# SSD group norm by four 32-column products with a root on 128x128, and earlier weight splits for the third group

## The chip, the cores and the metric

The kernel runs on one core of a Trainium2 chip. The time is that of one execution in device microseconds (us). The core has a matrix engine (TensorE, PE in the profile; its weight loads are PEld), VectorE (DVE), ScalarE (ACT), GpSimd (POOL) and SyncE (SP), which issues most DMAs. Each engine works its own instructions in order; semaphores let one wait for another.

## The reference

A trunk of two layers on x (1, 512, 1024): a gated short convolution, then a Mamba-2 mixer (SSD), each followed by a SwiGLU feed-forward, each with RMS norms before and after and a shift, scale and gate from c. The change lies in the SSD mixer. Cut to what matters:

```
z, xbc, dt_raw = split(h @ w_in)
xbc = silu(causal_depthwise_conv(xbc, conv_w) + conv_b)
xs, bm, cm = split(xbc)                 # 2048 channels, 8 groups x 128 states, twice
y = ssd_chunked(xs, dt, a, bm, cm) + d_skip * xs
y = y * silu(z)
y = rms_normalize(y.reshape(b, s, 8, 256)).reshape(b, s, 2048) * norm_g
return y @ w_out
```

The last norm is taken for each token over the 256 channels of one group: y / sqrt(mean(y*y) + eps).

## The kernel before

Activations lie with channels on the 128 partitions and the 512 tokens along the row. A float32 product is made of three products in a rounded format: each weight block (128x1024, `whl`) is split into a high part (ACT, a cast, L202) and a low part (DVE, the difference, L203), and PE multiplies high by high, high by low and low by high (`mm3`, L259 to L261), 24 matmuls of 512 columns for a block.

The SSD stage runs over 8 groups (`Group`). A group needs six blocks of projections: two of x (wx0, wx1), one of B and one of C (wbc0, wbc1), two of z (wz0, wz1). `load_w` loads two blocks in one staging tile `wst` (two such tiles) and splits each into one of four `whl` buffers; a buffer is free again when PE has used the block. The products for B, C and x go through a convolution (`conv4`: ACT's bias step and DVE's three steps L957, both on `cu`, then ACT's silu, L959, which makes `xs`, `bt`, `ct`), those for z through a silu alone (`zs`).

What the mixer does with them is cut into steps. `step_a` transposes xs and B (PE: `xtok`, `btokp`; DVE: `xw`, `xdt`) and multiplies C by B (`cb`, masked to `cbm`). `states` makes the chunk states `st` and their running sum `prev`. `e_sub` and `e_fin` make the decays in `csb` (DVE subtractions L1067, ACT's exponential, DVE's product with `cbm`). `step_cc` makes the two parts of y (PE: `yo` from `prev`, `yd` from `csb`), which DVE adds and gates to `yg`; their squares are summed in `accg`. `step_d` is the norm: a product of a 128x128 matrix of ones with `accg` sums over the partitions (`ssg`, the same sum on all 128 partitions), ACT takes the root (L1119), DVE the reciprocal (L1120) and multiplies both `yg` of the group by it (L1123).

PSUM has four banks for projections (`ip`) and four for all else (`ssg`, `xtok`, `btokp`, `cb`, `st`, `yo`, `yd`).

PE's order is written by hand: in pass g of the loop, the blocks of group g+1 stand between the steps of group g. For the first group and the projections of the second, the orders of ACT and DVE are written by hand too; from there on a scheduler sets them, by the priorities that instructions have from their place in the program. What stands in `tc.high_priority()` is taken ahead of the rest. In the passage between the two regimes, ACT and DVE split the blocks of the third group (`Group(2)`) while they finish the first and second.

Of the kernel before, what the change touches and what calls it, by code (L numbers as in the profile page):

```python
# [8 lines left out]
F32 = mybir.dt.float32  # L9
F32R = mybir.dt.float32r  # L10
AF = mybir.ActivationFunctionType
# [5 lines left out]
P = 128  # L17
T = 512
D = 1024
KD = D // P  # L20
DFF = 2816
NF = DFF // P
DIN = 2048
NH = 32
HD = 64
NG = 8
NCH = 4
# [8 lines left out]
def trunk_kernel(  # L36
# [9 lines left out]
    act, dve, pe, pool = nc.scalar, nc.vector, nc.tensor, nc.gpsimd  # L46
# [3 lines left out]
    dram = ctx.enter_context(tc.tile_pool(name="dram", bufs=1, space=DRAM))  # L50

    tmp = ctx.enter_context(tc.tile_pool(name="tmp", bufs=4))
# [7 lines left out]
    def aux_ps(name, shape=(P, T)):  # L60
        return ps.tile(list(shape), F32, tag="aux", name=name, bufs=4)

    def t2(name):
        return tmp.tile([P, T], F32, tag="t2", name=name, bufs=4)
# [4 lines left out]
    ones = consts.tile([P, P], F32, name="ones")  # L69
# [3 lines left out]
    eps_t = consts.tile([P, 1], F32, name="eps")  # L73
# [127 lines left out]
    def split_w(src, dst, nk):  # L201
        act.copy(dst[:, 0, :nk, :], src)  # L202
        dve.tensor_tensor(dst[:, 1, :nk, :], src, dst[:, 0, :nk, :].bitcast(F32), SUB)  # L203

    def load_w(srcs, nk=KD, k0=0, later=None):


        st = wst_p.tile([P, 8, 256], F32, tag="wst", name="wst")
        o = 0
        for m, c0, n in srcs:  # L210
            dma(st[:, :nk, o:o + n], m[k0 * P:(k0 + nk) * P, c0:c0 + n].rearrange("(k p) f -> p k f", p=P))
            o += n
        res = []
        for b in range(o // P):
            w = whl_p.tile([P, 2, 8, P], F32R, tag="whl", name="whl")
            sw = st[:, :nk, b * P:(b + 1) * P]
            if later is None:
                split_w(sw, w, nk)
            else:
                later.append((lambda sw=sw, w=w: act.copy(w[:, 0, :nk, :], sw),  # L220
                              lambda sw=sw, w=w: dve.tensor_tensor(w[:, 1, :nk, :], sw,
                                                                   w[:, 0, :nk, :].bitcast(F32), SUB)))
            res.append(w)
        return res
# [317 lines left out]
    wm_in, wm_out = m_w_in[0], m_w_out[0]  # L542

    with ExitStack() as ph:
# [96 lines left out]
        with tc.manual_schedule(engines={PE_ENGINE, mybir.EngineType.SP, mybir.EngineType.Activation,  # L641
# [122 lines left out]
            for name in OPENING.split():  # L764
                step(name)
            later = []
            next_cv = [load_w([(w_in0, (i + 1) * D + 2 * P, 256)], later=later) for i in range(2)]
            for hi, lo in later:
                hi()
# [20 lines left out]
        for jp in range(0, KD, 2):  # L790
            if jp == 0:
                pss = lead_ps[:4]
            else:
                ws = next_cv[0] + next_cv[1] if jp == 2 else [
                    w for i in range(2) for w in load_w([(w_in0, (i + 1) * D + jp * P, 256)])]
                pss = [in_chunk(w, h) for w in ws]
            us = [conv_mix_cv(jp + b, pss[b], pss[2 + b]) for b in range(2)]
            wb = load_w([(w_in0, jp * P, 256)]) if jp else None
            for b in range(2):
                a = act_tile(f"bu{jp + b}")  # L800
                conv_mix_b(us[b], in_chunk(wb[b], h) if jp else lead_ps[4 + b], a)
                acts.append(a)
            ada_next(2 if jp < 6 else 0)
            if jp == 4:
                put_gates(0)
                gg = make_gg(0, gg_tile)
                other_vectors(actp.tile([P, 8, P], F32, tag="a", name="rows2"))
# [57 lines left out]
    with ExitStack() as ph:  # L865
# [4 lines left out]

        cs_d = dram.tile([NH, T], F32, name="cs_d")
        ecs_d = dram.tile([NH, T], F32, name="ecs_d")

        dt_tok = consts.tile([P, NH, NCH], F32, name="dt_tok")
        cs_tok = consts.tile([P, NH, NCH], F32, name="cs_tok")
# [89 lines left out]
        class Group:  # L965
# [8 lines left out]
            def weights(self, i, later=None):  # L974
                g = self.g
                if i == 0:
                    self.wx = load_w([(wm_in, DIN + g * 256, 256)], later=later)
                elif i == 1:
                    self.wbc = load_w([(wm_in, 2 * DIN + g * P, P), (wm_in, 2 * DIN + D + g * P, P)],
                                      later=later)  # L980
                else:
                    self.wz = load_w([(wm_in, g * 256, 256)], later=later)

            def conv(self, i, pst):
                g = self.g
# [127 lines left out]
            def step_d(self):  # L1113

                g = self.g
                pt = aux_ps("ssg")
                pe.matmul(pt, ones, self.accg, start=True, stop=True)
                rg = t2("rg")
                act.activation(rg, pt, AF.Sqrt, bias=eps_t, scale=1.0 / 256)  # L1119
                dve.reciprocal(rg, rg)  # L1120
                for q in range(2):
                    y = ygs[2 * g + q]
                    dve.scalar_tensor_tensor(y, y, mng[:, 2 * g + q:2 * g + q + 1], rg, MUL, MUL)  # L1123
# [26 lines left out]
        with tc.manual_schedule(engines={PE_ENGINE, mybir.EngineType.Activation, mybir.EngineType.DVE}):  # L1150
            cur, nxt = Group(0), Group(1)
            later = []
# [365 lines left out]
```

## Time and profile before

| | us |
|---|---|
| median of 3 runs | 1379.9 |
| lowest, highest | 1378.26, 1380.02 |
| profiled execution | 1378.87 |
| its span, first to last instruction | 1377.0 |

The SSD stage lies between about 630 and 970 us of the span. A row of a timeline is start, duration, engine, line, operation, output<-inputs, form and count; in square brackets stand the idle time before it and what ended that. A row of the waits is who waited for whom: us in total, times, longest. In the chain of waits a row is start, length, engine, tile, line and count. `L959` and the like are lines of the kernel before.

### The profile page before, as it was taken

The page shows a single profiled execution, that of the slowest core. Times are in us where ns is not written, and L with a number is a line of the kernel's source. Part 1 is how long each engine was busy: PE and PEld are TensorE (multiplying, and loading weights), DVE is VectorE, ACT ScalarE, POOL GpSimd, SP SyncE. Part 2 cuts the span into 40 slices and gives each one's busy share as a digit, 9 for nine tenths or more (in the row PEclk, how much of TensorE's full clock was granted, in tenths as well). Part 3 has the DMA queues.
Part 4 walks back from the last instruction along what each step waited for, and adds up shares of the span by engine and source line. Part 5 has one row for each costly group of instructions (what it writes and reads, how often), then busy time and mean ns, then how long its engine had stood idle before and what let it go on. Part 6 is the DMA issues. An engine that isn't in the chain of part 4 may idle for free.

```text
span 1377.0 us, 17627 instructions
## 1 busy us (share of the span) xinstructions
PE 1353.4 (98%) x6973; PEld 1136.3 (83%) x6973; DVE 911.3 (66%) x1485; ACT 580.2 (42%) x875; POOL 1.5 (0%) x11
## 2 busy tenths in 40 slices
PE   8999999999999999999899999999999999999997
PEld 7788889888888888898778888888889888887886
DVE  5777757478775222669879888787675655334877
ACT  4432247222222211665655656543473222223754
POOL 0000000000000000000000000000000000000000
PEclk9999999999999999999989999999999999999999
DMA  9956670467683322514444324332233986423743
GB/s 314 318 182 218 228 238 24 136 215 274 215 283 106 130 93 69 149 33 144 120 139 128 91 89 138 108 107 92 92 122 134 343 276 244 134 69 128 249 163 118
DMA packets 163702, 222.09 MB, mean 161 GB/s; under 512 B 7060, under 2 KB 112164, under 8 KB 161188
## 3 DMA queue, kind: packets, MB, share of 16 engines
q1 hardware_dynamic: 159616, 208.20, 46.2%
q10 hardware_dynamic: 4004, 12.77, 2.9%
q8 instruction: 55, 0.90, 0.3%
q14 instruction: 27, 0.22, 0.0%
HBM read 207.17 MB, written 13.78 MB: 160 GB/s over the span
## 4 chain that ended last, share of the span: by engine, by line
PE 63%; DVE 3%; DMA 1%; ACT 0%; issue 0%; DVEq 0%; ACTq 0%
PE ip L259 11%; PE ip L261 11%; PE ip L260 11%; PE y L359 5%; PE y L360 5%; PE y L361 5%; PE li L259 2%; PE li L261 2%; PE li L260 2%; PE yd L1089 1%; PE yo L1082 1%; PE pa L1390 1%; PE pa L1391 1%; PE pb L1391 1%; PE pb L1390 1%; PE pb L1389 1%
## 5 line engine op out<-in xcount | busy, mean ns | idle before, releaser
L259 PE MATMUL ip<-h,whl 128*128 128x512 f32 x1096 | 434.6, 397 | 2.7 <-DVE cv L777 2.7
L261 PE MATMUL ip<-h,whl 128*128 128x512 f32 x1096 | 429.4, 392 | 6.6 <-DVE whl L203 6.6
L260 PE MATMUL ip<-h,whl 128*128 128x512 f32 x1096 | 428.4, 391 | 0.0
L261 PEld LDWEIGHTS ip<-h,whl 128*128 128x128 f32 x1096 | 206.8, 189 | 50.9 <-DVE whl L203 7.0
L259 PEld LDWEIGHTS ip<-h,whl 128*128 128x128 f32 x1096 | 206.8, 189 | 47.7 <-issue 5.1
L260 PEld LDWEIGHTS ip<-h,whl 128*128 128x128 f32 x1096 | 206.9, 189 | 43.3 <-issue 1.2
L202 ACT CAST whl<-wst 128x1024 fp32r<-128x1024 f32 (+1 forms) x163 | 152.2, 952 | 200.7 <-PE ip L261 148.2
L203 DVE TENSOR_TENSOR whl<-wst,whl 128x1024 fp32r<-128x1024 f32 (+1 forms) x163 | 177.0, 1102 | 62.4 <-ACT whl L202 62.0
L203 DVE TENSOR_TENSOR whlo<-wsto,whlo 128x1024 fp32r<-128x1024 f32 x46 | 56.3, 1224 | 96.2 <-ACT whlo L202 96.0
L126 DVE SCALAR_TENSOR_TENSOR ada_acc<-ada_st,csil,ada_acc 128x512 f32<-128x512 f32 x140 | 104.8, 749 | 22.6 <-DMA ada_st<-in_ada_w_dram 19.7
L202 ACT CAST whlo<-wsto 128x1024 fp32r<-128x1024 f32 x46 | 48.3, 1050 | 113.8 <-PE y L361 86.7
L259 PE MATMUL li<-h,whl 128*128 128x256 f32 x288 | 83.2, 289 | 0.0
L261 PE MATMUL li<-h,whl 128*128 128x256 f32 x288 | 81.6, 283 | 0.0
L260 PE MATMUL li<-h,whl 128*128 128x256 f32 x288 | 81.5, 283 | 0.0
L957 DVE SCALAR_TENSOR_TENSOR cu<-ip,cols,cu 128x511 f32<-128x511 f32 (+2 forms) x84 | 62.0, 741 | 12.9 <-ACT cu L954 12.7
L359 PE MATMUL y<-whlo,ff 128*128 128x512 f32 x176 | 68.6, 390 | 0.0
L361 PE MATMUL y<-whlo,ff 128*128 128x512 f32 x176 | 68.5, 389 | 0.0
L360 PE MATMUL y<-whlo,ff 128*128 128x512 f32 x176 | 68.5, 389 | 0.0
L259 PEld LDWEIGHTS li<-h,whl 128*128 128x128 f32 x288 | 55.3, 192 | 0.0
L260 PEld LDWEIGHTS li<-h,whl 128*128 128x128 f32 x288 | 55.2, 192 | 0.0
L261 PEld LDWEIGHTS li<-h,whl 128*128 128x128 f32 x288 | 55.1, 191 | 0.0
L359 PE MATMUL y<-whlo,ys 128*128 128x512 f32 x128 | 51.1, 399 | 0.0
(281 smaller groups left out, 1923.5 us busy)
## 6 DMA issues: line engine op xcount, KB each, us to landing
ada_st<-in_ada_w_dram SPq DMA_DIRECT2D x96, 512.0 KB, 5.9
wst<-in_f_w_in_dram SPq DMA_DIRECT2D x44, 1024.0 KB, 7.1
wst<-in_m_w_in_dram SPq DMA_DIRECT2D x14, 1024.0 KB, 5.4
tb<-in_f_w_out_dram SPq DMA_DIRECT2D x22, 512.0 KB, 7.3
td<-tb SPq DMA_DIRECT2D x11, 1024.0 KB, 5.0
wsto<-in_f_w_out_dram SPq DMA_DIRECT2D x10, 1024.0 KB, 4.9
wst<-in_m_w_in_dram SPq DMA_DIRECT2D x20, 512.0 KB, 5.1
wst<-in_a_w_in_dram SPq DMA_DIRECT2D x9, 1024.0 KB, 6.5
```

What stands on the lines that cost most here:

```text
L126: dve.scalar_tensor_tensor(acc, w, csil[:, k:k + 1], acc, MUL, ADD)
L202: act.copy(dst[:, 0, :nk, :], src)
L203: dve.tensor_tensor(dst[:, 1, :nk, :], src, dst[:, 0, :nk, :].bitcast(F32), SUB)
L259: pe.matmul(dst, w_at(w, 0, kk), a[:, 0, sl], start=start, stop=False)
L260: pe.matmul(dst, w_at(w, 0, kk), a[:, 1, sl], start=False, stop=False)
L261: pe.matmul(dst, w_at(w, 1, kk), a[:, 0, sl], start=False, stop=stop)
L359: pe.matmul(pst, a[:, 0, tk], wt[:, 0, kk, :], start=k == 0, stop=False)
L360: pe.matmul(pst, a[:, 0, tk], wt[:, 1, kk, :], start=False, stop=False)
L361: pe.matmul(pst, a[:, 1, tk], wt[:, 0, kk, :], start=False, stop=k == K - 1)
L957: dve.scalar_tensor_tensor(u[:, sft:], pst[:, :T - sft], w[3 - sft], u[:, sft:], MUL, ADD)
L1390: pe.matmul(acc[t], a[:, 0, sl], w[1], start=False, stop=False, skip_group_check=True)
L1391: pe.matmul(acc[t], a[:, 1, sl], w[0], start=False, stop=True, skip_group_check=True)
```

## The change

It has two parts. First, `step_d`: instead of one product of 512 columns there are four, each for 128 tokens (cc = 0 to 3). Each uses 32 columns of the ones and its own quarter of PE's columns, so that the sums of token quarter cc come out on partitions 32cc to 32cc+31 of one 128x128 tile. Root and reciprocal run on that tile `r4`. One partition of each quarter is then stored to DRAM (4x128, `rg_d`) and loaded back onto all 128 partitions as 512 tokens, both by DMAs that POOL issues. The load goes into `bt`, the tile of the group's own B, which `step_a` has done with; the next writer of that buffer is the silu of B two groups on. Second, the six splits of group 2 are put at high priority (`soon`).

```
-    def load_w(srcs, nk=KD, k0=0, later=None):
+    def load_w(srcs, nk=KD, k0=0, later=None, soon=False):
...
-                split_w(sw, w, nk)
+                with tc.high_priority() if soon else ExitStack():
+                    split_w(sw, w, nk)
...
+        rg_d = [dram.tile([NCH, P], F32, name=f"rg_d{g}") for g in range(NG)]
...
-                    self.wx = load_w([(wm_in, DIN + g * 256, 256)], later=later)
+                    self.wx = load_w([(wm_in, DIN + g * 256, 256)], later=later, soon=g == 2)
...
-                                      later=later)
+                                      later=later, soon=g == 2)
...
-                    self.wz = load_w([(wm_in, g * 256, 256)], later=later)
+                    self.wz = load_w([(wm_in, g * 256, 256)], later=later, soon=g == 2)
...
             def step_d(self):
...
-                pt = aux_ps("ssg")
-                pe.matmul(pt, ones, self.accg, start=True, stop=True)
-                rg = t2("rg")
-                act.activation(rg, pt, AF.Sqrt, bias=eps_t, scale=1.0 / 256)
-                dve.reciprocal(rg, rg)
+                pt = aux_ps("ssg", (P, P))
+                for cc in range(NCH):
+                    pe.matmul(pt[cc * 32:(cc + 1) * 32, :], ones[:, :32], self.accg[:, cc * P:(cc + 1) * P],
+                              start=True, stop=True, tile_position=(0, cc * 32))
+                r4 = tmp.tile([P, P], F32, tag="r4", name="r4", bufs=1)
+                act.activation(r4, pt, AF.Sqrt, bias=eps_t, scale=1.0 / 256)
+                dve.reciprocal(r4, r4)
+                pool.dma_start(rg_d[g], r4[0:P:32, :])
+                rg = self.bt
+                pool.dma_start(rg, rg_d[g].rearrange("c t -> (c t)").partition_broadcast(P))
                 for q in range(2):
                     y = ygs[2 * g + q]
                     dve.scalar_tensor_tensor(y, y, mng[:, 2 * g + q:2 * g + q + 1], rg, MUL, MUL)
```

On PE only `ssg` changes its place, and only for the first group: before it stood within the product of wx0 of group 2, eight matmuls in; now it stands behind that product, ahead of `xtok`. ACT and DVE are reordered from the end of the hand-written part on. Line numbers in rows of the changed kernel are 1 to 7 higher.

First place, DVE around the B and C blocks of group 2. In the kernel before (`whl_5662` and `whl_5665` are wbc0 and wbc1, `whl_5777` and `whl_5780` wz0 and wz1; the group norm's reciprocal stands seven rows further up):

```order
L957 SCALAR_TENSOR_TENSOR cu_5622<-ip_5597,cols3_91,cu_5622 128x510
L1056 TENSOR_TENSOR prev_5628<-prev_5628,dec_4979 128x256
L957 SCALAR_TENSOR_TENSOR cu_5622<-ip_5597,cols3_91,cu_5622 128x509
L1058 TENSOR_TENSOR prev_5628<-prev_5628,st01_5629 128x256
L1074 TENSOR_TENSOR csb_5401<-csb_5401,cbm_5590 128x1024
L1056 TENSOR_TENSOR prev_5628<-prev_5628,dec_4979 128x256
L203 TENSOR_TENSOR whl_5662<-wst_5659,whl_5662 128x1024
L1058 TENSOR_TENSOR prev_5628<-prev_5628,st2_5632 128x256
L203 TENSOR_TENSOR whl_5665<-wst_5659,whl_5665 128x1024
L203 TENSOR_TENSOR whl_5777<-wst_5775,whl_5777 128x1024
L203 TENSOR_TENSOR whl_5780<-wst_5775,whl_5780 128x1024
```

In the changed kernel wbc0 and wbc1 are `whl_5675` and `whl_5678`:

```order
L1102 TENSOR_TENSOR y1_5449<-yo_5418,ecsb_5174 128x384
L203 TENSOR_TENSOR whl_5675<-wst_5672,whl_5675 128x1024
L1103 SCALAR_TENSOR_TENSOR yg1_5448<-xs1_4991,dcol_94,yd_5431 128x512
L1069 TENSOR_SCALAR csb_5537<-csb_5537,cs_tok_4985 128x128
L1104 TENSOR_TENSOR yg1_5448<-yg1_5448,y1_5449 128x384
L1069 TENSOR_SCALAR csb_5537<-csb_5537,cs_tok_4985 128x128
L1105 TENSOR_TENSOR yg1_5448<-yg1_5448,zs1_5215 128x512
L1069 TENSOR_SCALAR csb_5537<-csb_5537,cs_tok_4985 128x128
L203 TENSOR_TENSOR whl_5678<-wst_5672,whl_5678 128x1024
L1069 TENSOR_SCALAR csb_5537<-csb_5537,cs_tok_4985 128x128 x5
L1112 TENSOR_TENSOR accg_5446<-accg_5446,sqg_5454 128x512
```

They moved from behind the reciprocal and the states of the second group to ahead of the first group's `accg`.

Second place, DVE at the second group's `xdt`, before:

```order
L957 SCALAR_TENSOR_TENSOR cu_5449<-ip_5373,cols3_91,cu_5449 128x509
L1067 TENSOR_SCALAR csb_5524<-csb_5524,cs_tok_4977 128x128 x7
L1023 TENSOR_TENSOR xw_5569<-xtok_5570,dte_tok_4978 128x512
L1025 TENSOR_TENSOR xdt_5568<-xtok_5570,dt_tok_4976 128x512
L1023 TENSOR_TENSOR xw_5569<-xtok_5577,dte_tok_4978 128x256
```

and changed, where `whl_5790` is wz0 of group 2:

```order
L1025 TENSOR_TENSOR xw_5582<-xtok_5583,dte_tok_4986 128x512
L959 SCALAR_TENSOR_TENSOR cu_5457<-ip_5381,cols3_91,cu_5457 128x509
L203 TENSOR_TENSOR whl_5790<-wst_5788,whl_5790 128x1024
L1027 TENSOR_TENSOR xdt_5581<-xtok_5583,dt_tok_4984 128x512
L1025 TENSOR_TENSOR xw_5582<-xtok_5590,dte_tok_4986 128x256
```

A convolution step and a split now stand between the first `xw` and the first `xdt`. On ACT, the cast of the same block now stands ahead of the silu that makes `ct`, and waits for PE to have done with wx0.

Third place, DVE from the second group's reciprocal to the product with it, in the changed kernel (before, the reciprocal was followed by one `xw` and then by both products):

```order
L1124 RECIPROCAL r4_5853<-r4_5853 128x128
L203 TENSOR_TENSOR whl_6005<-wst_5999,whl_6005 128x1024
L1025 TENSOR_TENSOR xw_5909<-xtok_5910,dte_tok_4986 128x512
L1027 TENSOR_TENSOR xdt_5908<-xtok_5910,dt_tok_4984 128x512
L1025 TENSOR_TENSOR xw_5909<-xtok_5917,dte_tok_4986 128x256
L1027 TENSOR_TENSOR xdt_5908<-xtok_5917,dt_tok_4984 128x512
L959 SCALAR_TENSOR_TENSOR cu_5902<-ip_5877,cols3_91,cu_5902 128x511
L1039 TENSOR_TENSOR cbm_5930<-cb_5931,mask_82 128x512
L959 SCALAR_TENSOR_TENSOR cu_5902<-ip_5877,cols3_91,cu_5902 128x510
L1130 SCALAR_TENSOR_TENSOR yg2_5769<-yg2_5769,cols1_89,bt_4996 128x512
L1130 SCALAR_TENSOR_TENSOR yg3_5777<-yg3_5777,cols1_89,bt_4996 128x512
```

The later groups have the same order here. On POOL's queue stand only the two DMAs of each group.

## The prediction

> **What bounds the kernel now.** I read the page first, then TensorE's (PE's) waits, then the timeline around the largest of them.
>
> ```profile
> PE 1353.4 (98%) x6973; PEld 1136.3 (83%) x6973; DVE 911.3 (66%) x1485; ACT 580.2 (42%) x875; POOL 1.5 (0%) x11
> PE ip L261 <- DVE whl L203: 6.6, 1, 6.6
> PE cb L1036 <- DVE xdt L1025: 0.7, 1, 0.7
> ```
>
> PE is busy for 98% of the span, so an edit elsewhere pays only where PE waits. In the whole SSD stage there are two waits of any size: 6.6 us on a weight split and 0.7 us on a bank that DVE empties. The timeline shows the first, and a window (busy time of PE, its loads, DVE, ACT and POOL, then the granted clock) what came behind it.
>
> ```profile
> 684.56 0.39 PE L260 MATMUL ip<-h,whl 128*128 128x512 f32 x1
> 691.53 0.79 PE L261 MATMUL ip<-h,whl 128*128 128x512 f32 x1 [6.58 <-DVE whl L203]
> 697.24 0.41 PE L259 MATMUL ip<-h,whl 128*128 128x512 f32 x1
> 697.96 0.39 PE L259 MATMUL ip<-h,whl 128*128 128x512 f32 x1
> 698.64 0.39 PE L259 MATMUL ip<-h,whl 128*128 128x512 f32 x1
> 691.50:697.30 5.80, 5.77 (x14) 4.51 (x15) 4.92 (x6) 1.66 (x3) 0.00 (x0) 0.50 0.54 171
> ```
>
> Undisturbed, three matmuls take 698.64 - 697.96 = 0.68, so one starts each 0.227 us. The matmul due at 684.79 starts at 691.53: 6.74 us lost. The next 13 start at half speed (granted clock 0.50) until 697.24: 5.71 us for work of 2.95, so 2.76 more. **The wait costs 9.5 us.** What it waits for stands in the queues of ACT and DVE:
>
> ```profile
> 678.93 1.98 ACT L202 CAST whl<-wst 128x1024 fp32r<-128x1024 f32 x2
> 679.68 3.35 DVE L1120 RECIPROCAL rg<-rg 128x512 f32<-128x512 f32 x1
> 690.25 1.22 DVE L203 TENSOR_TENSOR whl<-wst,whl 128x1024 fp32r<-128x1024 f32 x1
> ```
>
> ACT had made the high part by 681. DVE had the time but did other things first, among them the group norm's reciprocal (3.35 us), and made the low part at 690.25.
>
> **The priority.** In the new order both low parts stand ahead of the sum that ends the norm's squares (the first place of the order above), so this wait goes: -9.5. What is late next? The split of the first z block, wz0, now stands ahead of `xdt` (second place), and `cb` has to wait for `xdt`, as the 0.7 us row says. These rows give the lengths:
>
> ```profile
> 674.51 1.03 PE L1019 MATMUL xtok<-ident,xs 128*128 128x128 f32 x8
> 675.14 0.69 DVE L1023 TENSOR_TENSOR xw<-xtok,dte_tok 128x512 f32<-128x512 f32 x1 [3.13 <-PE xtok L1019]
> 675.75 0.68 DVE L1025 TENSOR_TENSOR xdt<-xtok,dt_tok 128x512 f32<-128x512 f32 x1
> 676.35 0.41 DVE L1023 TENSOR_TENSOR xw<-xtok,dte_tok 128x256 f32<-128x256 f32 x1
> 676.58 1.13 PE L1036 MATMUL cb<-ct,bt 128*128 128x128 f32 x8 [0.71 <-DVE xdt L1025]
> 666.72 1.04 ACT L202 CAST whl<-wst 128x1024 fp32r<-128x1024 f32 x1
> 668.76 1.22 DVE L203 TENSOR_TENSOR whl<-wst,whl 128x1024 fp32r<-128x1024 f32 x1
> 669.90 0.74 DVE L957 SCALAR_TENSOR_TENSOR cu<-ip,cols,cu 128x509 f32<-128x509 f32 x1
> 670.56 1.45 DVE L1067 TENSOR_SCALAR csb<-csb,cs_tok 128x128 f32<-128x128 f32 x7
> 719.27 0.86 PE ssg L1117 x2
> 725.62 0.87 PE xtok L1019 x8
> 726.82 0.89 PE cb L1036 x8
> 746.72 1.90 PE yd L1089 x32
> ```
>
> From start to start DVE takes 0.61 for `xw`, 0.60 for `xdt`, 1.14 for a split, 0.66 for a convolution step. Now the new order at this place, on the old clock. The old ssg (0.86) sat inside the x block's product; it moves behind it, so the product ends at 674.51 - 0.86 = 673.65. There wz0's buffer comes free and ACT casts it until 674.7; behind that cast in ACT's queue stand `ct`, both silus of z, the root and the next bias step, and `ct` waits for the last convolution step anyway. PE goes on with ssg (0.35, below) and transposes at 674.00; `xw` starts 0.63 later as before, 674.63; then 0.61, 0.66, 1.14 and 0.60: `xdt` ends at 677.64 and `cb` starts some 0.15 behind, 677.8, instead of 676.58. So PE loses 1.2 there, waiting from 675.2 (the transposes before `cb` take 726.82 - 725.62 = 1.2) for 2.6 us. What does such a wait do to the clock? The nearest row is a wait of 2.69 us in layer 0:
>
> ```profile
> 64.39 0.47 PE L259 MATMUL ip<-h,whl 128*128 128x512 f32 x1 [2.69 <-DVE cv L777]
> 65.87 0.63 PE L259 MATMUL ip<-h,whl 128*128 128x512 f32 x1
> 69.26 0.39 PE L261 MATMUL ip<-h,whl 128*128 128x512 f32 x1
> 65.60:69.30 3.70, 3.70 (x11) 2.87 (x10) 3.70 (x7) 0.72 (x1) 0.00 (x0) 0.54 1.09 354
> ```
>
> Eight matmuls then took 3.39 instead of 1.82: 1.6 lost at clock 0.54. After the 0.7 us wait no such row follows. I take 1.6, the bounds being 0 and 2.8. (The Trainium skill, TensorE: Matmul & The Clock Gate, Why this matters for your kernels, warns only of idle gaps above about 3 us; by that the new wait would cost no clock and the sum below would be 1.6 better. The row at 64.39 goes against it, and I follow the row.)
>
> **Four products of 32 columns.** The old product costs PE 0.86 us (ssg row). The new one is eight records of 128 columns. At full width eight such records cost 0.89 (cb row), at 64 columns 1.90/32 = 0.059 each, so 0.48. The 32-column form occurs in layer 0:
>
> ```profile
> 23.80 1.08 PE L184 MATMUL ada_pe<-ada_st,rows 128*32 128x128 f32 x32
> 24.81 0.96 PE L714 MATMUL li<-h,whl_l 128*128 128x512 f32 x3
> 745.23 1.50 PE L1082 MATMUL yo<-ct,prev 128*128 128x128 f32 x12
> 748.55 0.50 PE L259 MATMUL ip<-h,whl 128*128 128x512 f32 x1
> 748.89 0.39 PE L260 MATMUL ip<-h,whl 128*128 128x512 f32 x1
> ```
>
> 1.01/32 = 0.032 each, so 0.25 for eight; the matmul behind the 64-column `yd` held PE for 0.34 instead of 0.23, so I add 0.1: 0.35, a saving of 0.5 (bounds -0.03 and 0.61). The Trainium skill (TensorEngine Tiling (Array Packing), Key Properties) says that a change of tiling mode drains the engine; the 0.11 us behind `yd` is what that can be here, and without it each product would be 0.1 cheaper. In the first group the saving is already in the 1.2 above; seven others stand between dense products: -3.5.
>
> **Root and reciprocal.** The root runs on 128x128 instead of 128x512 (0.69 us, L1119), the reciprocal too: at a quarter of 3.35, 0.84. DVE gains 2.5 us per group, ACT some 0.4; PE waits for neither, so I cost it at nothing directly. It is the cover for what follows.
>
> **Two DMAs per group.** Both `yg` multiplications now wait for a store and a broadcast load on POOL's queue, which holds nothing else from here on; behind them in DVE's queue stand the last convolution step, the two products of `csb`, wz's splits and the `prev` sums that `yo` needs. The trace shows no DMA from POOL. Nearest rows:
>
> ```profile
> cs_d<-csb SPq DMA_DIRECT2D x1, 64.0 KB, 3.1
> ecsb<-ecs_d ACTq DMA_DIRECT2D x16, 256.0 KB, 5.9
> out_dram<-x SPq DMA_DIRECT2D x8, 256.0 KB, 2.0
> r<-in_f_w_out_dram SPq DMA_DIRECT2D x11, 256.0 KB, 3.0
> ```
>
> Store and load together lie between 2.0 + 3.0 = 5 and 3.1 + 5.9 = 9 us; I take 7. How much is covered? In a later group, on the old clock:
>
> ```profile
> 721.61 0.69 ACT L1119 ACTIVATE rg<-ssg,eps 128x512 f32<-128x512 f32 x1
> 738.49 0.42 DVE L1058 TENSOR_TENSOR prev<-prev,st 128x256 f32<-128x256 f32 x1
> ```
>
> The root ends near 721.9, the reciprocal near 722.75. PE's transposes begin near 724.9, `xw` at 725.5, and the six operations behind it (third place of the order) bring DVE to `yg` near 729: 6.3 us of cover. Then DVE has some 10 us of work to the last `prev` sum, at 739 instead of 738.49, and `yo` wants it at 745: another 6 us. So up to about 12 us the round trip is hidden, and I cost it at nothing; each us beyond costs PE one, in six groups. In the first group the reciprocal ends near 681.7 and `yg` is reached near 687.6; with a round trip of 7 `prev` is complete near 694, 2 to 3 us before `yo`.
>
> **The sum.** -9.5 + 1.2 + 1.6 - 3.5 = -10.2 us. The profiled execution took 1378.87 us (span 1377.0, 1.9 around it), 1.0 below the median of the three runs, 1379.9. That is 1368.7 on its own scale and 1369.7 on the median's; I take 1369.
>
> **The rivals.**
>
> Clean: `xdt` comes in time because DVE reaches it sooner than I reckon, or PE's new wait stays below what trips the clock. For it: the 0.7 us wait left the clock at full. Against it: the split ahead of `xdt` cannot start before ACT's cast, which waits for PE. It gives -9.5 - 0.7 - 8 x 0.5 = -14.2, 1365; with the lowest price of the product 1364.
>
> The wait moves: the high casts of wx1, wbc and wz0 now stand early in ACT's queue and each waits for PE to leave a buffer, so squares, `bt` and `ct` come later; if one of them also holds PE 3 to 5 us with a slow clock, the gain is cut to 4 to 6 us: 1373 to 1375. For it: ACT works its queue strictly in order, and the 2.6 us above come about in just this way. Against it: I find the accumulated squares done near 672, before PE asks at 673.65.
>
> Slower: the round trip on POOL's queue exceeds about 12.5 us. Then DVE stands at `yg` in every group, `prev` comes after PE wants it, and each wait also slows the clock by 1.6: six groups times (1.6 and the excess) eat the 10.2 us at once. At 16 us it gives 6 x (3.7 + 1.6) - 10.2 = +22, 1401. For it: two transfers in series, of a kind that the trace does not show. Against it: 9 us from the rows. The Trainium skill has a rule for it (SBUF — State Buffer, Two separate sides): GpSimd writes a DMA's descriptors through a port that a DVE operation in a two-port mode locks. Such operations here could be the `csb` subtractions (seven in 1.45 us), and in later groups none stands between reciprocal and `yg`; so I give that rule little weight.
>
> No change: the priority doesn't move the splits or the small products cost the full 0.89. The order speaks against the first, the ada_pe row against the second: 1379.
>
> **How the numbers follow.** Forecast 0.52, clean 0.20, the wait moves 0.14, no change 0.06, slower 0.08. The range 1363 to 1376 holds the first three. A measurement of this kernel tells about 0.2% (2.8 us) from no change; faster by more than that 0.86, within 0.06, slower 0.08.
>
> **What would show it.** PE's 6.6 us wait on `whl` is gone, with the clock at full after it; a wait of 2 to 3 us at `cb` of the second group on `xdt` stands instead; ssg takes 0.3 to 0.4 us; `yg` waits 0 to 3 us for POOL's load, and PE's `yo` never waits for `prev`. A wait at `yo` in several groups, or a load landing over 12 us after the reciprocal, would make it wrong.

## The result and the profile after

| | before | after |
|---|---|---|
| median, us (6 runs each) | 1379.96 | 1372.03 |
| lowest, highest | 1378.26, 1380.86 | 1370.37, 1373.23 |
| profiled execution, us | 1378.87 | 1372.71 |
| its span, us | 1377.0 | 1370.9 |

The ratio is 0.9945 (95% interval 0.9933 to 0.9956): 7.9 us less, faster by more than the 0.2% that can be told. The forecast was 1369, its range 1363 to 1376. Three executions among those of the experiments below took 3182 to 5874 us, and the ratios leave them out.

PE's waits of the changed kernel, in the SSD stage alone (655 to 960 us; in total, times, longest):

```profile
PE cb L1038 <- DVE xdt L1027: 2.9, 1, 2.9
PE ssg L1120 <- DVE accg L1112: 0.2, 1, 0.2
```

The 6.6 us on the split are gone, and the wait at `cb` has grown from 0.7 to 2.9 us. (Lines of the new kernel stand one or two, in the norm three to seven, further down.) The reader should not compare spans of two profiled executions to judge a stage: PE issues the same matmuls in the same order in both kernels, but for `ssg`, so one can set the same matmul of both side by side. The first and the last `yo` frame the stage; of the view of that tile, the row of before and that of after (shortest, median, longest in ns, then first and last start):

```profile
L1082 PE MATMUL yo<-ct,prev x96: 270/275/275, 653.8 to 960.3; 128*128 128x128 f32 x96
```

```profile
L1084 PE MATMUL yo<-ct,prev x96: 270/275/275, 655.4 to 953.5; 128*128 128x128 f32 x96
```

From 306.5 to 298.1: the stage gained 8.4 us, and 0.5 more at the last `ssg`, which stands behind the last `yo`. The first `yo` came 1.6 us later than before, though nothing ahead of it was changed; that is the scatter of single executions, part of which the last section explains. The terms, read in the same way:

```profile
675.55 0.43 PE L1120 MATMUL ssg<-accg,ones 128*32 128x128 f32 x8 [0.19 <-DVE accg L1112]
680.24 1.13 PE L1038 MATMUL cb<-ct,bt 128*128 128x128 f32 x8 [2.92 <-DVE xdt L1027]
...
689.80 0.39 PE L261 MATMUL ip<-h,whl 128*128 128x512 f32 x1
690.02 0.39 PE L262 MATMUL ip<-h,whl 128*128 128x512 f32 x1
...
693.00 0.39 PE L260 MATMUL ip<-h,whl 128*128 128x512 f32 x1
```

| term | rows (before; after) | measured | forecast |
|---|---|---|---|
| `cb` of group 1 later | 676.58 - 653.8; 680.24 - 655.4 | +2.0 | +1.2 |
| clock behind it | 684.56 - 676.58; 689.80 - 680.24 | +1.6 | +1.6 |
| the stall on the split | 697.24 - 684.56; 693.00 - 689.80 | -9.5 | -9.5 |
| six later `ssg`, to the last `yo` | 960.3 - 697.24; 953.5 - 693.00 | -2.6 | -3.0 |
| the seventh, behind the last `yo` | 969.23 - 967.76; 961.92 - 960.91 | -0.5 | -0.5 |
| sum | | -8.9 | -10.2 |

The matmul of the split, at 691.53 before, stands at 690.02 now, 0.22 behind its predecessor and without a wait. (The terms are rounded; from the unrounded rows the sum is -8.9.) Of the -2.6, 0.55 is a wait of `ssg` for `accg` in group 5 that is gone (groups are counted from 0, as in the code); the prediction had no term for it. The six products themselves saved 0.31 each; the seventh saved more, since before it took 1.02 us and the others 0.87.

### The profile page after: what moved, and what is told of

Read it like the earlier page. It is cut to its first block, busy times and chain, and to the rows that moved or that the text cites. A ratio compares the mean times of both kernels' runs of the same rounds, so it can differ in the third digit from the quotient of the medians.

```text
span 1370.9 us, 17793 instructions
## 1 busy us (share of the span) xinstructions
PE 1349.5 (98%) x7021; PEld 1133.5 (83%) x7021; DVE 895.2 (65%) x1485; ACT 577.2 (42%) x875; POOL 10.8 (1%) x27
## 4 chain that ended last, share of the span: by engine, by line
PE 63%; DVE 2%; DMA 1%; ACT 1%; issue 0%; DVEq 0%; ACTq 0%
PE ip L260 11%; PE ip L262 11%; PE ip L261 11%; PE y L360 5%; PE y L362 5%; PE y L361 5%; PE li L260 2%; PE li L262 2%; PE li L261 2%; PE yd L1091 1%; DMA wst<-in_m_w_in_dram 1%; PE yo L1084 1%; PE pa L1397 1%; PE pb L1397 1%; PE pb L1396 1%; PE pz L1397 1%
```

## Experiments

Times stand beside runs of the kernel before on the same chip; the last column is the stage from first to last `yo` in the profiled execution (306.5 in before).

| kernel | us | before, us | ratio (95%) | stage |
|---|---|---|---|---|
| e1 priority only | 1373.56 | 1378.55 | 0.9959 (0.9945 to 0.9972) | 299.6 |
| e2 norm only | 1370.25 | 1378.55 | 0.9945 (0.9932 to 0.9959) | 296.2 |
| e3 priority without z | 1369.71 | 1378.55 | 0.9934 (0.9921 to 0.9946) | 294.7 |
| e4 three more hops | 1373.81 | 1378.55 | 0.9971 (0.9961 to 0.9981) | 297.4 |
| e5 norm only, wide reciprocal | 1381.61 | 1378.91 | 1.0024 (1.0013 to 1.0035) | 307.6 |
| e6 priority for B and C only | 1368.98 | 1378.91 | 0.9933 (0.9920 to 0.9945) | 295.0 |
| e7 the changed kernel again | 1373.31 | 1378.91 | 0.9962 (0.9949 to 0.9974) | 298.1 |
| e8 same quarter | 1382.20 | 1378.91 | 1.0030 (1.0019 to 1.0042) | 306.3 |
| e9 priority for the second block | 1367.73 | 1378.41 | 0.9923 (0.9903 to 0.9943) | 294.5 |
| e10 norm only again | 1371.33 | 1378.41 | 0.9945 (0.9925 to 0.9965) | 296.4 |

**e1, the priority alone.** `step_d` as in the kernel before, `soon` kept.

> The splits of group 2 first, the norm as before (one product of 512 columns, root and reciprocal on 128x512). Theory A (the two parts add: the priority takes the 6.6 us stall and brings the 2.9 us wait at cb; the norm saves only TensorE's shorter product): the 3.05 us that the seven later products saved are missing, 1372.0 + 3.1 = 1375 us; wait at cb 2.9 as in the changed kernel, no wait on a split. Rival B (the short reciprocal is what lets the priority work): the 3.35 us reciprocal stands ahead of another split of group 2 and a wait of 2 us or more on whl comes back: 1377 to 1380.

Measured: 5.0 us below before, stage 299.6, no wait on a split in the passage. A holds in this, that the priority takes the stall without the norm; that the two parts add, e2 refutes. `cb` waited 2.50 us, and here the clock stayed whole behind it, which spared this profile some 1.6 us; the stage is 1.5 us longer than with both parts.

**e2 and e10, the norm alone.**

```
-    ..., later=later, soon=g == 2)
+    ..., later=later, soon=False)
```

> The new norm, no priority. Theory A (the priority alone takes the stall): the first split of group 2's B and C block still comes after PE wants it, a wait of 4 us or more on whl with half clock behind it stays, less 2.5 us for the reciprocal: 1374 to 1376. Rival B (the norm alone takes most of it, since the short reciprocal and the yg products that now come later leave VectorE free for the split): that split comes within 1 us of when PE wants it, and the second one of the block is late by 2 to 3 us instead: 1370 to 1373.

Measured: 8.3 us below before, and the stage shorter than with both parts (296.2 against 298.1). B holds in its mechanism and its time. VectorE's and PE's rows of e2:

```profile
677.93 0.95 DVE L1124 RECIPROCAL r<-r 128x128 f32<-128x128 f32 x1
682.06 1.22 DVE L203 TENSOR_TENSOR whl<-wst,whl 128x1024 fp32r<-128x1024 f32 x1
684.88 1.42 DVE L1130 SCALAR_TENSOR_TENSOR yg<-yg,cols,bt 128x512 f32<-128x512 f32 x2 [1.60 <-DMA bt<-rg_d]
690.45 0.50 PE L262 MATMUL ip<-h,whl 128*128 128x512 f32 x1 [1.38 <-DVE whl L203]
```

The first split of the block begins 3.2 us behind the reciprocal's end, ahead of `yg`, and is in time; only the second is late, by 1.4 us where B had 2 to 3. So the stall that the prediction gave to the priority goes without it. e10 was run to see whether that was luck:

> The norm alone once more, beside the former. Theory A (its time is that of the first run): 1369 to 1371, waits of 0.7 us at cb and 1.4 us on the second block's split, full clock behind both. Rival B (the first run was a lucky one): 1372 or more.

1371.33, 0.3 above A's range, and stage 296.4: the stage of the first run was not luck. The waits were 0.7 us at `cb` and 1.6 on the second split.

**e5, which part of the norm does it.** As e2, with the root and the reciprocal widened:

```
-                r4 = tmp.tile([P, P], F32, tag="r4", name="r4", bufs=1)
-                act.activation(r4, pt, AF.Sqrt, ...)
-                dve.reciprocal(r4, r4)
+                rw = t2("rg")
+                r4 = rw[:, :P]
+                act.activation(rw (4 x 128), pt repeated four times, AF.Sqrt, ...)
+                dve.reciprocal(rw, rw)
```

> The new norm without the priority, but with root and reciprocal widened to 128x512 again (the 128 columns four times over; only the first 128 are stored), the round trip kept. Theory A (the short reciprocal frees VectorE for the first split of the block in time): with 3.35 instead of 0.95 us that split falls behind when PE wants it, and in this order behind the yg products too; PE waits 5 us or more on whl and the clock drops behind it: 1375 to 1379. Rival B (it is enough that the yg products come later, behind the round trip): as the norm alone, 1370 to 1372.

Measured: 2.7 us slower than before, A, and 2.6 us beyond its range. VectorE's rows, then PE's:

```profile
679.80 3.35 DVE L1126 RECIPROCAL rg<-rg 128x512 f32<-128x512 f32 x1
...
689.27 1.42 DVE L1132 SCALAR_TENSOR_TENSOR yg<-yg,cols,bt 128x512 f32<-128x512 f32 x2 [0.81 <-DMA bt<-rg_d]
...
690.93 1.22 DVE L203 TENSOR_TENSOR whl<-wst,whl 128x1024 fp32r<-128x1024 f32 x1
```

```profile
692.21 0.80 PE L262 MATMUL ip<-h,whl 128*128 128x512 f32 x1 [7.15 <-DVE whl L203]
```

The stall is back whole, 7.15 us. So the later `yg` alone does not do it: with the round trip but a long reciprocal, the scheduler puts the split behind `yg`, and `yg` waits for the load. Beside this round trip the short reciprocal is needed. It is 2.4 us shorter, but in e2 the split begins 3.2 us behind the reciprocal's end and here 7.8: most of the difference comes from the order that the scheduler makes with the longer operation. (The root was widened too, from 0.37 to 0.69 us on ACT; the two were not taken apart.) Whether a short reciprocal would do without the round trip was not tried. Five more waits of about 0.5 us on splits came up in later groups.

**e3, e6, e9: which splits should come first.** In e3 the z block is split in the ordinary order, in e6 the x block too, and in e9 of B and C only the second block has the priority.

```
e3: -                    self.wz = load_w(..., later=later, soon=g == 2)
    +                    self.wz = load_w(..., later=later)
e6: the same edit at self.wx and at self.wz
e9: as e6, and
-                with tc.high_priority() if soon else ExitStack():
+                with tc.high_priority() if soon and b == 1 else ExitStack():
```

> As the changed kernel, but the z block of group 2 is split in the ordinary order; the split between xw and xdt goes. Theory A (that split makes the new wait at cb): xdt comes 1.14 us earlier, the wait falls from 2.9 to 1.8 us, and if the half clock behind it goes too, 1372.0 - 1.1 - 1.7 = 1369.2; if it stays, 1370.9. Rival B (the z split is wanted early): PE waits for whl at the first z block, and the time is 1372 or more.

> The new norm, and the priority for the B and C block of group 2 alone. Theory A (the norm alone leaves one wait, 1.4 us on the second split of that block; moved ahead, both low parts fall into 3 us in which VectorE waits for the transposes): no wait on whl, 0.7 us at cb: 1.4 us below the norm alone, 1368 to 1369. Rival B (each split moved ahead costs a wait at cb, as in the changed kernel): a wait of 1.5 us or more at cb and, when the clock drops, 1.6 more: 1370 to 1373.

> The new norm, and the priority for the second block alone of group 2's B and C. Theory A (what the norm alone leaves is one wait of 1.4 us on that block, whose split needs no place ahead of xdt or of the squares, only one ahead of the yg products): split directly behind the first block's, near 683, wanted near 689: no wait on whl in the SSD stage, 0.7 us at cb, half clock nowhere in the stage: 1.4 us below the norm alone run beside it, 1368 to 1369. Rival B (the list of the later groups changes with it and a wait comes up elsewhere): as the norm alone or more, 1370 to 1373.

PE's row at `cb` in e3, then in e9:

```profile
676.87 1.16 PE L1038 MATMUL cb<-ct,bt 128*128 128x128 f32 x8 [1.40 <-ACT ct L961]
```

```profile
675.34 1.13 PE L1038 MATMUL cb<-ct,bt 128*128 128x128 f32 x8 [0.71 <-DVE xdt L1027]
```

e3: A. Without the z split ahead of `xdt` the wait falls from 2.9 to 1.4 us, what ends it is now `ct`, and the clock stays whole: 294.7 for the stage. e6: no wait on a split, as A said, but 1.6 us at `cb` for `ct`, as B said, since the two splits stand ahead of the last convolution step for `ct`; both halves are right, and with a whole clock it comes out where A put it. e9: A. In the stage one wait of 0.7 us is left, which was there before, and both splits stand in one row ahead of `yg`:

```profile
682.58 2.35 DVE L203 TENSOR_TENSOR whl<-wst,whl 128x1024 fp32r<-128x1024 f32 x2
685.65 1.41 DVE L1130 SCALAR_TENSOR_TENSOR yg<-yg,cols,bt 128x512 f32<-128x512 f32 x2 [0.71 <-DMA bt<-rg_d]
```

e9 is the fastest of all, 1367.7: clearly below the kernel before, and beside e10 on the same chip 3.6 us less, of which the stage shows 1.9. The changed kernel did not run on that chip; e9's interval lies below that of e7 but overlaps that of the changed kernel's first run. By time alone e3, e6 and e9 can't be told apart.

**e4, a longer round trip.** Three copies from DRAM to DRAM between store and load:

```
+                pool.dma_start(rg_e[g][0], rg_d[g])
+                pool.dma_start(rg_e[g][1], rg_e[g][0])
+                pool.dma_start(rg_e[g][2], rg_e[g][1])
```

> As the changed kernel, with three more copies of the 2 KB from DRAM to DRAM in the round trip, each about 2.3 us (581 ns on POOL and 1.7 to landing), so 6.9 us more from reciprocal to yg. Theory A (VectorE stands at yg where it stood): the slack between the last prev and yo, 4.1, 3.1, 3.9, 4.7, 2.9 and 4.8 us in groups 1 to 6, is used up, PE waits 2 to 4 us in each for prev, 17.9 in all, and some 1.6 each for the clock: 1399. Rival B (the order adapts: in the new order yg stands nine rows later on VectorE, behind the prev sums): no wait at yo, 1371 to 1374.

Measured: 1373.8, PE never waits at `yo`. B holds, though not to the letter: in the pass of group 1 `yg` moved behind all `prev` sums, in that of group 2, where the trip from reciprocal to `yg` took 15.3 us, `yg` stands ahead of the last one, which is done 1.9 us before `yo`. The order was made anew, so VectorE doesn't stand where it stood. But one place has no later work to put in front: the last group. Rows of the chain of waits that ends in the first transpose of the next stage, in e4 (start, length, step):

```profile
960.91 0.96 DVE r L1125
...
972.58 5.33 DMA bt<-rg_e
...
979.95 1.15 DVE whlo L203
...
981.11 4.92 DMA wst<-in_f_w_in_dram
...
990.99 8.80 DMA wst<-in_f_w_in_dram
...
999.81 0.63 ACT whl L202
```

PE's wait for the next norm (us in total, times, longest):

```profile
PE xtr L461 <- ACT xn L452: 3.3, 2, 3.0
```

`yg` of the last group holds up a split of the output weights, that split holds a staging buffer, the buffer the next weights, and these stand ahead of the next norm in ACT's queue: PE waits 3.0 us at `xtr`, where the changed kernel does not wait.

**e7, the changed kernel again.**

> The changed kernel once more, beside the others on the same chip. Theory A (the half clock behind a wait of 2.5 to 3.2 us comes in some executions and not in others): 1370 to 1373, with the 2.9 us wait at cb; behind it and behind the wait in layer 0 the clock may be whole or half. Rival B (the half clock follows from the length of the wait): half clock behind both, since both are as long as before.

1373.3, 0.3 above A's range; A holds on the clock. PE's rows, then two windows (busy times, granted clock, DMA share, GB/s), the first from e7 and the second from the changed kernel's first profile:

```profile
675.72 0.43 PE L1120 MATMUL ssg<-accg,ones 128*32 128x128 f32 x8 [1.86 <-DVE accg L1112]
680.41 1.13 PE L1038 MATMUL cb<-ct,bt 128*128 128x128 f32 x8 [2.92 <-DVE xdt L1027]
...
682.00:685.00 3.00, 3.00 (x15) 2.46 (x14) 3.00 (x6) 2.97 (x4) 0.22 (x1) 1.00 0.00 0
```

```profile
682.00:685.00 3.00, 3.00 (x9) 2.32 (x8) 3.00 (x7) 2.97 (x4) 0.40 (x1) 0.52 0.00 0
```

The same wait of 2.92 us, once with half clock behind it and once without. That the stage took 298.1 us both times is chance: e7 lost at `ssg` what the other lost to the clock.

**e8, all four products on the same 32 columns.**

```
-                    pe.matmul(pt[cc * 32:(cc + 1) * 32, :], ..., tile_position=(0, cc * 32))
+                    pe.matmul(pt[:32, cc * P:(cc + 1) * P], ..., tile_position=(0, 0))
```

> As the changed kernel, but all four products use the first 32 of PE's columns and write one row of 512 sums (on 32 partitions); root and reciprocal run on 32x512, so VectorE has its 3.35 us again. Theory A (a product with 32 columns of weights is cheap in itself): the eight records of a ssg take 0.43 us from first start to last end as in the changed kernel. Rival B (products on different quarters run beside each other): 0.86 to 0.9 us. In time: A 1371 to 1373, B some 2.3 us more, like the priority alone, 1373 to 1375.

PE around the product of group 1, in before, in the changed kernel and in e8:

```profile
718.88 0.39 PE L261 MATMUL ip<-h,whl 128*128 128x512 f32 x1
719.11 1.02 PE L1117 MATMUL ssg<-accg,ones 128*128 128x512 f32 x2
...
720.20 0.40 PE L260 MATMUL ip<-h,whl 128*128 128x512 f32 x1
```

```profile
714.60 0.39 PE L262 MATMUL ip<-h,whl 128*128 128x512 f32 x1
714.91 0.43 PE L1120 MATMUL ssg<-accg,ones 128*32 128x128 f32 x8
715.27 0.50 PE L260 MATMUL ip<-h,whl 128*128 128x512 f32 x1
715.61 0.39 PE L261 MATMUL ip<-h,whl 128*128 128x512 f32 x1
```

```profile
712.32 0.39 PE L262 MATMUL ip<-h,whl 128*128 128x512 f32 x1
712.64 1.06 PE L1120 MATMUL ssg<-accg,ones 128*32 128x128 f32 x8
...
713.96 0.40 PE L261 MATMUL ip<-h,whl 128*128 128x512 f32 x1
```

From the matmul ahead to the second behind, less two undisturbed 0.227: 0.87, 0.56 and 1.19 us. B, with 1.06 us where it had 0.86 to 0.9: a product with 32 columns of weights is not cheap in itself; four on different quarters of the array run beside each other (0.43 us for the eight records against 1.06). e8 also writes all sums to the same 32 partitions, so the columns of the array and the place of the output are not told apart. The time of e8, 1382, is much above what either theory gave, since the order changed with it: the 3.34 us reciprocal is back and brought a wait of 3.7 us in the pass of group 2, on a split of group 3, which has no priority, with half clock behind it.

## Why the prediction was right, and where it was off

The direction, the place and the largest term held: the stall went with the slow clock behind it (-9.5 of -9.5), a wait of 2 to 3 us came up at `cb` of group 1 for `xdt`, and the clock behind it cost 1.6. That the clock term came out to the tenth was luck: in e7 the same wait cost no clock. Point by point:

- **The new wait was mis-sized.** `cb` came 2.0 us late instead of 1.2. The step that failed is "I find the accumulated squares done near 672, before PE asks at 673.65", and with it "`xw` starts 0.63 later as before". The chain of waits that leads to `cb`, in the changed kernel:

```profile
657.95 9.62 DMA wst<-in_m_w_in_dram
...
671.53 1.04 ACT whl L202
...
672.59 1.23 DVE whl L203
...
674.80 0.60 DVE accg L1112
...
678.36 1.13 DVE whl L203
679.50 0.61 DVE xdt L1027
...
680.24 1.13 PE cb L1038 x8
```

  and ACT's row of the first cast:

```profile
667.67 1.05 ACT L202 CAST whl<-wst 128x1024 fp32r<-128x1024 f32 x1 [10.33 <-DMA wst<-in_m_w_in_dram]
```

  The high casts of B and C stand at the head of ACT's queue, and the first waits 10.3 us for its weights to land, until 667.67; the squares stand behind the second cast, the sum behind its split, and the convolution steps, `xw` and `xdt` behind the sum. `accg` is done at 675.4, which is 673.8 with the 1.6 us by which this execution ran late taken off, and not 672. So `ssg` came some 0.3 late and `xw`, behind the convolution steps, another 0.5. The prediction had this as its rival "the wait moves", though there the casts wait for PE to leave a buffer and not for weights, and set it aside on the number that was wrong. In e7, where PE came there 1.5 us earlier, the weights landed no earlier (the cast began at 667.84), and PE waited 1.86 us at `ssg` in place of 0.19.
- **The products** saved 0.31 each, not 0.5 (the 0.55 that the six brought besides is the wait of group 5 in the kernel before, which the prediction passed over when it counted two waits in the stage): the eight records hold PE for 0.56 us instead of 0.35. The price of entering and leaving them was taken as 0.1; measured, the first starts 0.31 behind the matmul ahead instead of 0.227, and the second matmul behind comes 0.34 after the first, so some 0.2 for both, and the eight themselves take 0.36, not 0.25. The mechanism (less than the 512 columns) was right. The 0.11 behind the product, which the prediction read behind `yd` as what a change of tiling mode can be, is mostly something else: behind `cb`, which has the full width, the step from the first to the second matmul is 0.32.

```profile
722.05 1.06 PE L1038 MATMUL cb<-ct,bt 128*128 128x128 f32 x8
722.86 0.48 PE L260 MATMUL ip<-h,whl 128*128 128x512 f32 x1
723.18 0.39 PE L261 MATMUL ip<-h,whl 128*128 128x512 f32 x1
```

- **The round trip** was taken as 7 us from reciprocal to `yg`. For the norm of group 1, in the pass of group 2, it was 7.3; the last row is that of the last group:

```profile
719.33 0.95 DVE L1124 RECIPROCAL r<-r 128x128 f32<-128x128 f32 x1 [3.41 <-ACT r L1123]
727.60 1.42 DVE L1130 SCALAR_TENSOR_TENSOR yg<-yg,cols,bt 128x512 f32<-128x512 f32 x2 [1.98 <-DMA bt<-rg_d]
737.10 0.41 DVE L1060 TENSOR_TENSOR prev<-prev,st 128x256 f32<-128x256 f32 x1
740.62 1.50 PE L1084 MATMUL yo<-ct,prev 128*128 128x128 f32 x12
973.62 1.42 DVE L1130 SCALAR_TENSOR_TENSOR yg<-yg,cols,bt 128x512 f32<-128x512 f32 x2 [3.36 <-DMA bt<-rg_d]
```

  VectorE waits for 2 us in the pass of group 2, and `prev` is complete 3.1 us ahead of `yo`, not 6 (2.9 to 4.8 in the passes of groups 1 to 6). Costing it at nothing was right, the slack was half of what was reckoned, and e4 shows that it isn't used up as the prediction feared: the order moves. The rival "slower" was worked out for six groups; the place where e4's longer trip did cost, 3 us, is the norm of the last group, which the prediction left out. There VectorE waits longest in the changed kernel too, 3.4 us, where the prediction gave 0 to 3.
- **Who took the stall.** The prediction gave all of it to the priority and costed the short reciprocal "at nothing directly". The total was near, the reason incomplete: either part alone takes the stall (e1, e2; of 6.6 us e2 leaves 1.4), e5 shows that of the norm it is the length of root and reciprocal, and with the norm in place the priority of all six splits takes more at `cb` than it gives: `cb` comes 2.0 us later, and the wait on the second split that it removes was 1.4 and 1.6. The stages differ by more, 298.1 with the priority against 296.2 and 296.4 without, but most of that is the half clock, or in e7 the wait at `ssg`. By time alone the two can't be told apart: the ratio is 0.9945 for the changed kernel, for e2 and for e10. The prediction's own rows put the 3.35 us reciprocal ahead of the late split; what was not asked is where the split would stand with 0.95 in its place and `yg` waiting for a load.
- **Between 8.9 and 7.9.** The stage gained 8.9 us in the profiled executions, the medians 7.9, and the two profiled executions as a whole 6.2: 1.6 were lost ahead of the stage, the rest behind it. Outside the stage the kernel is not changed, and single executions differ there by 1 to 3 us (below); what of the 1 us between stage and medians is that, and what the range of the medians, stays open.

## What to carry to other kernels

A stall behind a long operation on a shared engine can be taken away by moving the late work ahead or by making the long operation short; try each alone before both, since here the two did not add. Before work is given priority, look at what its first instruction waits for: in a queue worked in order, all that stands behind inherits that wait, here the landing of weights. Where a scheduler makes the order, as here, a longer latency in the middle of a loop can be moved around (e4); look for its price in the last turn, behind which nothing is left to move.

## What the runs showed of the hardware

**The clock behind a wait of 2.5 to 3.2 us differs from one execution to the next.** A wait of this length stands in layer 0 in all profiles but e10 (for `cv`), and at `cb` in some:

| profile | layer 0: wait, us | clock behind | `cb`: wait, us | clock behind |
|---|---|---|---|---|
| before | 2.69 | half | 0.71 | whole |
| after | 2.65 | half | 2.92 | half |
| e1 | 2.81 | half | 2.50 | whole |
| e2 | 2.76 | whole | 0.71 | whole |
| e3 | 3.21 | whole | 1.40 | whole |
| e4 | 2.57 | whole | 2.50 | half |
| e5 | 2.59 | half | 0.71 | whole |
| e6 | 2.59 | half | 1.61 | whole |
| e7 | 2.55 | half | 2.92 | whole |
| e8 | 2.48 | whole | 2.50 | whole |
| e9 | 2.71 | whole | 0.71 | whole |
| e10 | 2.35 | whole | 0.71 | whole |

With the 2.97 us at `xtr` in e4 (clock whole) these are, the start of the program aside, seventeen waits between 2.48 and 3.21 us. Eight were followed by half clock, for about 3 us (6 in one case), and the longest was not; the three from 3.69 us up (6.58, 7.15, 3.69) all were. Nor need one wait be that long: near the end of every kernel but e1 stand two of 0.5 to 1.3 us, one matmul apart, and behind them the clock was half for about 3 us in e2, e3 and e7 (0.87 and 0.76 us in e7, then 0.50 from 1259 to 1262) and whole in the others. A dip of 3 us costs about 1.6, so one kernel's executions differ by that much at each such place. This is most of the scatter ahead of the stage: at the end of layer 0's dip the changed kernel's profiled execution was 1.2 us later than before's, at the same matmul, and e2's 1.7 earlier. The Trainium skill (TensorE: Matmul & The Clock Gate, What's actually happening) describes a free-running window of 3.4 us that the clock is decided by. The trace agrees in this, that the same wait of 2.92 us goes both ways, as it would if the phase decided; the window itself no run here shows. The bound that the Trainium skill gives (TensorE: Matmul & The Clock Gate, Why this matters for your kernels), no idle gaps above about 3 us, is too wide by these rows: 2.50 us was enough once.

**Products on different quarters of the array overlap, and switching to them costs 0.1 us at most** (0.56 us against 1.19 on the same quarter, in e8). The Trainium skill (TensorEngine Tiling (Array Packing), Key Properties) has both: tiles work independently, and a change of mode drains the engine. The trace agrees with the first. For the second it leaves little: the product starts 0.31 behind the matmul ahead, where the full-width `xtok` starts 0.23 behind it, and the second matmul behind it comes 0.34 after the first, where it is 0.32 behind `cb`.

**A broadcast of 512 sums through DRAM takes some 6 us.** The two DMAs of a group in the changed kernel, by the page (KB each, median us from issue to landing):

```profile
bt<-rg_d POOLq DMA_DIRECT2D x8, 256.0 KB, 4.1
rg_d<-r POOLq DMA_DIRECT2D x8, 2.0 KB, 1.7
```

5.8 us for both, and 7.3 in the row of the pass of group 2 above (719.33 + 0.95 to 727.60), with VectorE's own queue in it.
